# A one-core encoder kernel: the loads at the head of the RWKV-7 scan put in a hand-made order, and the last part of one gram step written earlier

## The chip, the cores and the metric

The kernel runs on one core of a Trainium2 chip. The metric is the device time of one execution in microseconds. Three runs of the kernel before took 2218.02, 2221.55 and 2223.59 us; the median is 2221.55 us. The profiled execution took 2221.22 us, and its program, from the first instruction to the last, spans 2219.4 us. All times of the trace are counted from the start of that span.

## What is computed

The reference is a two-layer encoder on 512 tokens of width 1024. Each layer is a half-step SwiGLU, a token mixer and another half-step SwiGLU, each followed by a layer norm. Layer 0 mixes by neighbourhood attention, layer 1 by a bidirectional RWKV-7 scan. The change lies in the mixer of layer 1:

```python
r = xr @ w_rkv[0]; k = xk @ w_rkv[1]; v = xv @ w_rkv[2]
g = jax.nn.sigmoid(xg @ g1) @ g2
...
def step(state, inp):
    r_t, w_t, k_t, v_t, a_t, b_t = inp
    sa = jnp.einsum('zbhij,zbhj->zbhi', state, a_t)
    state = state * w_t[..., None, :] + sa[..., None] * b_t[..., None, :] + v_t[..., None] * k_t[..., None, :]
    return state, jnp.einsum('zbhij,zbhj->zbhi', state, r_t)
_, ys = lax.scan(step, zeros, xs)      # one scan per direction z
...
return ((y + bonus) * g) @ w_out
```

`xr`, `xk`, `xv` and `xg` are token-shifted mixes of the input.

## The kernel before, in words

The work is fp32. The 16 heads of 64 channels are handled as 8 pairs (`hp`, 0 to 7), each 128 partitions wide. A scan over 512 tokens is cut into 8 chunks of 64 (`NC`), both directions `z` run side by side, and the recurrence inside a chunk is replaced by small matrices: products of keys and receptances ("grams"), the inverse of a triangular matrix per chunk, and then a chain over the 8 chunks that carries the state.

**Threads and slots.** `Scan.run` goes through slots `n` from -2 to 7. A slot holds threads, which are Python generators, and a string in the table `SEQ` says in which order their next parts are written out. For TensorE (PE), ScalarE (ACT) and VectorE (DVE) this written order is the order on the engine. The letters that matter here:

- `f0`, `f1`: `front`, the scaled receptances, keys and decays of pair n+3 in direction 0, or pair n+2 in direction 1. They write the tiles `ar0`/`ar1` (L1346, L1353) and `bk0`/`bk1` (L1360, L1363). One `ar` tile per direction exists, so the next pair's write to it has to wait until everything has read the old one.
- `g0`, `g1`: `grams`, six parts per pair and direction: for each half `q` of the chunks a PE part (L1385, masked out of PSUM by DVE at L1390), and then for each head `h` a part that copies pieces of the result to `qd` and `qc` on ACT (L1394, L1396) and issues two DMAs: L1397 moves a block of the unit `xs` to `az`, and L1398 puts a block of `ar` in its place in `xs`. The second one is what frees `ar`.
- `t0`, `t1`: `tails`, PE transposes of `bk` (L1408) that go to `tb` by ACT (L1409).
- `v`: `values`, `v = xv @ w_v` for one pair, one 128-row piece of the contraction per part (`a<-xv,wv` at L1063). `weigh` (L1431) loads the pair's weights `wv`.
- `r`: `receptances`, `r = xr @ w_r` for seven pairs, two pieces of the contraction per part (L1063, into the PSUM tiles `y` and `m` in turn), a copy by ACT (L1178) and a store to DRAM (L1179). Its inputs `xr` lie in `az2`, `xs8` and `xs9`, which nothing else uses yet; its weights lie in `xs4` to `xs7` and in two `vt` tiles. The first part of the thread (before slot -2) issues the loads of `xr` (L1148) and of the first weights.
- `q`: `gates`, four of the products with `g2`, each copied by ACT (L1441) into one of the tiles `yh`, `yt`, `gate`, `bon` and stored to DRAM by L1442.
- `b`: `bonus`; DVE L1448 reads the receptances and writes `kz`, PE makes a row sum of it, DVE L1453 reads that out of the PSUM tile `a` into `bon`. The tile `a` has two banks; `front` uses it too (L1327, and L270 to L272 for `a<-ah,a2u`).
- `i`, `k`, `j`: `invert` (one DVE transposition of `qd`, L1484, and then 62 POOL instructions, L1491 and L1493), `inverted` (DVE L1503 and L1512, which need POOL's result) and `merge` (PE L1524 and L1531). `c`, `d`: the chain over the chunks and its outputs.

**DMA order.** Every DMA here is issued by SP (SyncE). SP's order isn't written by hand: a scheduler puts the DMAs in line by its own estimate of when each is ready. `behind(x)` forces what stands inside to come after instruction `x` in that line. The eight loads of `xv` (256 KB each, L1161) are issued in the first `r` part of slot -2, after `wv` (L1431).

Of the kernel before, what the change touches and what calls it, by code (L numbers as in the profile page):

```python
# [18 lines left out]
P = 128  # L19
D = 1024  # L20
S = 512
FF = 2816
NF = FF // P
ND = D // P
# [34 lines left out]
}  # L59
SEQ = {  # L60
# [997 lines left out]
class Scan:  # L1058
# [76 lines left out]
    def receptances(self):  # L1135

        nc = self.nc
        one = lambda ap: ap.rearrange("p a b c d -> p (a b c d)")
        az = self.az[2].rearrange("p a b c -> p (a b c)")
        xr = [h[:, i * S : (i + 1) * S] for h, n in ((az, 4), (one(self.units[-2][0]), 2), (one(self.units[-1][0]), 2)) for i in range(n)]  # L1140
        w = {}

        def load(hp, ap):
            w[hp] = ap.rearrange("p (c f) -> p c f", c=ND)
            nc.sync.dma_start(w[hp], self.w_r[:, hp * P : (hp + 1) * P].rearrange("(c p) f -> p c f", p=P))

        def chunk(c):
            nc.sync.dma_start(xr[c], self.dram["xr"][:, c, :])  # L1148

        for n in ("mask", "onesb"):  # L1150
            nc.sync.dma_start(getattr(self, n), self.consts[n])
        chunk(0)
        for hp, i in zip(WR_FIRST, (4, 5, 6, 7)):
            load(hp, one(self.units[i][0]))
            if hp == WR_FIRST[0]:
                for c in range(1, ND):
                    chunk(c)
                self.weigh(0)
                yield
                for c in range(ND):  # L1160
                    nc.sync.dma_start(self.xv[:, c, :], self.dram["xv"][:, c, :])  # L1161
        for _ in range(2):
            self.unit()
        rest = [hp for hp in range(1, ND) if hp not in WR_FIRST]
        order = WR_FIRST + tuple(rest)
        while rest:
            pair, rest = rest[:2], rest[2:]
            vt = self.tile("vt", [P, NC, 2, 2, CH], 2)
            for i, hp in enumerate(pair):
                load(hp, one(vt)[:, i * D : (i + 1) * D])  # L1170
        for i, hp in enumerate(order):
            pr = self.k.bank("ym"[i % 2])
            for c in range(ND):
                self.wide(pr, w[hp][:, c, :], xr[c], c == 0, c == ND - 1)
                if c % 2 and c < ND - 1:
                    yield
            t = self.tile(("yh", "yt")[hp % 2], [P, S])
            nc.scalar.activation(t, pr, AF.Copy)  # L1178
            nc.sync.dma_start(self.dram["rkv"][0][:, hp, :], t)  # L1179
            if hp == order[-1]:  # L1180
                self.clear(2)
            yield
# [250 lines left out]
    def gates(self):  # L1433

        nc = self.nc
        for j, c in enumerate(range(ND - GATES, ND)):
            pg = self.k.bank("ym"[j % 2])
            for i, n in enumerate((P, 32)):
                nc.tensor.matmul(pg, self.g2[:n, i, j * P : (j + 1) * P], self.hidden[:n, i, :], start=i == 0, stop=i == 1)
            t = self.tile(("yh", "yt", "gate", "bon")[j], [P, S])  # L1440
            nc.scalar.activation(t, pg, AF.Copy)  # L1441
            nc.sync.dma_start(self.dram["g"][:, c, :], t)  # L1442
            yield

    def bonus(self, hp):
# [379 lines left out]
```

## Time and profile before

| | |
|---|---|
| three runs, us | 2218.02, 2221.55, 2223.59 (median 2221.55) |
| profiled execution, us | 2221.22 (span of the program 2219.4) |
| PE busy | 2180.0 us, 98% of the span |
| DVE, ACT, POOL busy | 1051.1, 957.7, 1413.1 us |
| mean granted TensorE clock | 0.994 |
| head of the scan | about 1414 to 1520 us (slots -2 and -1) |
| first slots with the chain over chunks | from about 1520 us |

The page's busy line says how long an engine had an instruction in work. The view of waits says, per waiting instruction line, what ended the wait, for how long in total, how often, and the longest one. A row of the timeline is: start, duration, engine, line, operation, output<-inputs by the program's tile names without their numbers, form, and how many equal instructions the row joins; in brackets how long the engine was idle before it and what released it. SPq rows are DMA issues by SP. An fp32 matmul instruction stands as two rows' worth of counts in the timeline (`x4` for two instructions). A row of the view by windows gives PE's busy time in that stretch, the count, the granted TensorE clock, the DMA engines' share and GB/s.

### The profile page before, as it was taken

The page shows a single profiled execution, that of the slowest core. Times are in us where ns is not written, and L with a number is a line of the kernel's source. Part 1 is how long each engine was busy: PE and PEld are TensorE (multiplying, and loading weights), DVE is VectorE, ACT ScalarE, POOL GpSimd, SP SyncE. Part 2 cuts the span into 40 slices and gives each one's busy share as a digit, 9 for nine tenths or more (in the row PEclk, how much of TensorE's full clock was granted, in tenths as well). Part 3 has the DMA queues.
Part 4 walks back from the last instruction along what each step waited for, and adds up shares of the span by engine and source line. Part 5 has one row for each costly group of instructions (what it writes and reads, how often), then busy time and mean ns, then how long its engine had stood idle before and what let it go on. Part 6 is the DMA issues. An engine that isn't in the chain of part 4 may idle for free. (4 is left out here: it accounts for less than half of the span.)

```text
span 2219.4 us, 35156 instructions
## 1 busy us (share of the span) xinstructions
PE 2180.0 (98%) x13834; PEld 1704.9 (77%) x13834; DVE 1051.1 (47%) x1526; ACT 957.7 (43%) x1678; POOL 1413.1 (64%) x1232
## 2 busy tenths in 40 slices
PE   9999999999999999999999999999999999999998
PEld 8888888887888888888888875445666657888886
DVE  3223355276433333633333588334788645333345
ACT  3333335377343333433333444336777533333333
POOL 5988855554487787488878542044777723887853
PEclk9999999999999999999999999999999999999999
DMA  7444463432344444454444645854444653444443
GB/s 206 147 155 144 142 223 100 136 89 91 103 138 143 150 147 150 150 181 146 143 138 142 209 130 181 277 142 129 128 129 120 194 162 102 151 142 142 138 171 123
DMA packets 350690, 329.15 MB, mean 148 GB/s; under 512 B 48491, under 2 KB 277483, under 8 KB 350525
## 3 DMA queue, kind: packets, MB, share of 16 engines
q1 hardware_dynamic: 350524, 326.91, 47.7%
q8 instruction: 109, 1.79, 0.3%
q14 instruction: 57, 0.46, 0.1%
HBM read 262.59 MB, written 47.74 MB: 140 GB/s over the span
## 5 line engine op out<-in xcount | busy, mean ns | idle before, releaser
L266 POOL TENSOR_TENSOR w<-raw,w 128x1024 fp32r<-128x1024 f32 (+1 forms) x202 | 499.7, 2475 | 255.4 <-ACT w L265 248.9
L270 PE MATMUL bank<-xT,w 128*128 128x512 f32 x1424 | 555.5, 390 | 0.0
L271 PE MATMUL bank<-xT,w 128*128 128x512 f32 x1424 | 554.2, 389 | 0.0
L272 PE MATMUL bank<-xT,w 128*128 128x512 f32 x1424 | 554.1, 389 | 0.0
L265 ACT ACTIVATE w<-raw 128x1024 fp32r<-128x1024 f32 (+1 forms) x206 | 217.3, 1057 | 318.0 <-PE bank L272 122.3
L477 DVE SCALAR_TENSOR_TENSOR ar<-bank,tmp 128x512 f32<-128x512 f32 x88 | 60.9, 692 | 563.9 <-PE bank L272 554.0
L272 PEld LDWEIGHTS bank<-xT,w 128*128 128x128 f32 x1424 | 267.3, 188 | 55.5
L270 PEld LDWEIGHTS bank<-xT,w 128*128 128x128 f32 x1424 | 267.4, 188 | 54.8
L271 PEld LDWEIGHTS bank<-xT,w 128*128 128x128 f32 x1424 | 267.4, 188 | 54.1
L871 PE MATMUL bank<-wx,an 128*128 128x512 f32 x792 | 187.3, 389 | 0.0
L1491 POOL TENSOR_TENSOR tm<-qs,zs 128x126 f32<-128x126 f32 (+22 forms) x248 | 105.5, 425 | 108.6 <-issue 48.3
L871 PEld LDWEIGHTS bank<-wx,an 128*128 128x128 f32 x792 | 148.7, 188 | 30.8
L871 PE MATMUL bank<-w,ring 128*128 128x512 f32 x720 | 168.8, 390 | 2.6 <-POOL w L266 2.6
L266 POOL TENSOR_TENSOR wx<-ra,wx 128x512 fp32r<-128x512 f32 x132 | 167.1, 1295 | 3.0 <-ACT wx L265 3.0
L266 DVE TENSOR_TENSOR ring<-ar,ring 128x1024 fp32r<-128x1024 f32 x44 | 121.3, 2757 | 90.2 <-ACT ring L265 90.1
L871 PEld LDWEIGHTS bank<-w,ring 128*128 128x128 f32 x720 | 134.9, 188 | 31.9 <-POOL w L266 3.6
L475 ACT ACTIVATE tmp<-bank 128x512 f32<-128x512 f32 x88 | 52.6, 598 | 231.5 <-PE bank L272 231.4
L1493 POOL TENSOR_TENSOR zs<-zs,tm 128x126 f32<-128x126 f32 (+22 forms) x248 | 113.9, 459 | 19.4
L265 ACT ACTIVATE wx<-ra 128x512 fp32r<-128x512 f32 x132 | 82.7, 633 | 79.0 <-PE bank L871 65.2
L266 POOL TENSOR_TENSOR w<-late,w 128x1024 fp32r<-128x1024 f32 x30 | 77.4, 2586 | 58.2 <-ACT w L265 58.2
L266 POOL TENSOR_TENSOR ring<-raw,ring 128x1024 fp32r<-128x1024 f32 x24 | 58.9, 2464 | 81.0 <-ACT ring L265 81.0
L270 PE MATMUL bank<-xT,ring 128*128 128x256 f32 (+1 forms) x304 | 87.3, 296 | 2.8 <-ACT xT L265 1.9
(315 smaller groups left out, 3714.3 us busy)
## 6 DMA issues: line engine op xcount, KB each, us to landing
raw<-in_ffn_w_in_dram SPq DMA_DIRECT2D x176, 512.0 KB, 3.9
ra<-in_ffn_w_out_dram SPq DMA_DIRECT2D x44, 1024.0 KB, 5.0
late<-d_late SPq DMA_DIRECT2D x34, 512.0 KB, 5.5
late<-in_ffn_w_out_dram SPq DMA_DIRECT2D x28, 512.0 KB, 4.4
raw<-in_w_qkv_dram SPq DMA_DIRECT2D x24, 512.0 KB, 3.9
d_late<-ts SPq DMA_DIRECT2D x44, 256.0 KB, 3.3
d_late<-ra SPq DMA_DIRECT2D x44, 256.0 KB, 2.0
xs<-ar SPq DMA_DIRECT2D x64, 128.0 KB, 2.4
```

Of the source, the lines that this page charges most:

```text
L265: self.hi = self.nc.scalar.activation(h, raw, AF.Copy).ins
L266: self.lo = (eng or self.nc.vector).tensor_tensor(l, raw, h.bitcast(F32), ALU.subtract).ins
L270: nc.tensor.matmul(out, wh, xh, start=start, stop=False)
L271: nc.tensor.matmul(out, wh, xl, start=False, stop=False)
L272: nc.tensor.matmul(out, wl, xh, start=False, stop=stop)
L475: nc.scalar.activation(s, pg, AF.Silu)
L477: nc.vector.scalar_tensor_tensor(raw[:, 3:7:3] if j else raw[:, 0:8:7], halves_of(pu), 0.5, halves_of(s), ALU.mult, ALU.mult)
L871: self.nc.tensor.matmul(acc, lhs, u[:, i], start=bool(first) and m == 0, stop=last and m == 2, skip_group_check=more)
L1491: nc.gpsimd.tensor_tensor(tv, qs[:, s, 0:s].rearrange("p (a o) -> p a o", o=1).broadcast_to([P, s, n]), zs[:, s : s + 1, c0:].broadcast_to ...
L1493: nc.gpsimd.tensor_tensor(zs[:, 0:s, c0:], zs[:, 0:s, c0:], tv, ALU.add)
```

## The change

Three edits. In `gates`, the four results go to the tiles `yt`, `gate`, `bon`, `yh` in this order (before: `yh`, `yt`, `gate`, `bon`), and the stores of the second to fourth are forced behind the last DMA remembered in `self.asked`. In `receptances`, the thread has one more stop: the load of `wv` and the eight loads of `xv` are issued in a part of their own, forced behind the first store of `gates`, and the last of the `xv` loads is what `gates` then stays behind. In `SEQ`, slot -2 calls that part between the first two `q`, takes all four parts of the first receptance product together before the second half of pair 0's grams, and slot -1 writes the last part of pair 1's `g0` right behind the part before it, where it stood much later, after the `g1` parts.

```diff
 SEQ = {
-    -2: "f1 q q f1 q f1 q g0 v f1 f1 f1 g0 l g0 r r g0 g0 v r g1 g1 g1 v r g1 v g1 g1 v t0 r g0 r r v f1 b r r t0 v r l v t1 "
+    -2: "f1 q r q f1 q f1 q g0 v f1 f1 f1 g0 l g0 r r r r g0 g0 v g1 g1 g1 v g1 v g1 g1 v t0 r g0 r r v f1 b r r t0 v r l v t1 "
        "i f0 r f0 r r v b f0 r r f0 r r t1 f0 r r f0",
-    -1: "f1 v g0 k f1 g0 g0 v r r f1 k r f1 f1 r j f1 g0 l l r g1 r n r g0 g1 f0 g1 j g1 f0 f1 r t0 g1 g1 n g0 v t0 v "
+    -1: "f1 v g0 k f1 g0 g0 v r r f1 k r f1 f1 r j f1 g0 l l r g1 r n r g0 g0 g1 f0 g1 j g1 f0 f1 r t0 g1 g1 n v t0 v "
        "f0 v v b f0 v t1 i f0 t1 f0 v n v r b",
...
             if hp == WR_FIRST[0]:
                 for c in range(1, ND):
                     chunk(c)
-                self.weigh(0)
                 yield
-                for c in range(ND):
-                    nc.sync.dma_start(self.xv[:, c, :], self.dram["xv"][:, c, :])
+                with self.k.behind(self.asked):
+                    self.weigh(0)
+                    for c in range(ND):
+                        self.asked = nc.sync.dma_start(self.xv[:, c, :], self.dram["xv"][:, c, :]).ins
+                yield
...
-            t = self.tile(("yh", "yt", "gate", "bon")[j], [P, S])
+            t = self.tile(("yt", "gate", "bon", "yh")[j], [P, S])
             nc.scalar.activation(t, pg, AF.Copy)
-            nc.sync.dma_start(self.dram["g"][:, c, :], t)
+            with self.k.behind(*[self.asked] if j else ()):
+                self.asked = nc.sync.dma_start(self.dram["g"][:, c, :], t).ins
             yield
```

What moves, engine by engine. POOL's and DVE's orders stay as they were. On SP at the head, before (tile numbers are kept here: `xs4_` to `xs9_` are units, `gh` holds k and iv of pair 1):

```order
L1148 DMA xs9_10657<-d_xr_71 128x512 x2
L1431 DMA wv_10693<-in_w_rkv_dram 128x8x128
L1442 DMA d_g_73<-yh_10650 128x512
L1442 DMA d_g_73<-yt_10649 128x512
L1442 DMA d_g_73<-gate_10652 128x512
L1290 DMA gh_10380<-d_k_69 128x512
L1292 DMA gh_10380<-d_iv_78 64x512
L1442 DMA d_g_73<-bon_10651 128x512
L1161 DMA xv_10639<-d_xv_72 128x512 x3
L1397 DMA az0_10668<-xs0_10655 64x4x64 x2
L1161 DMA xv_10639<-d_xv_72 128x512 x5
L1145 DMA xs5_10662<-in_w_rkv_dram 128x8x128
```

and with the change:

```order
L1148 DMA xs9_10657<-d_xr_71 128x512 x2
L1445 DMA d_g_73<-yt_10649 128x512
L1433 DMA wv_10703<-in_w_rkv_dram 128x8x128
L1162 DMA xv_10639<-d_xv_72 128x512 x8
L1445 DMA d_g_73<-gate_10652 128x512
L1445 DMA d_g_73<-bon_10651 128x512
L1445 DMA d_g_73<-yh_10650 128x512
L1399 DMA az0_10668<-xs0_10655 64x4x64
L1292 DMA gh_10380<-d_k_69 128x512
L1294 DMA gh_10380<-d_iv_78 64x512
L1399 DMA az0_10668<-xs0_10655 64x4x64
L1145 DMA xs5_10662<-in_w_rkv_dram 128x8x128
```

The loads of `xv` pass three of the gate stores, the loads into `gh` and the two moves to `az0`; the same DMAs as before stand ahead of `xs5`. On PE at the same place, before (`xs_10666` is `xs8`, `xs_10657` is `xs9`, `xs_10642` holds the first weights, `ar_10595` is direction 0 and `ar_10722` direction 1):

```order
L1063 MATMUL y<-az_10670,xs_10642 64x512 x8
L1385 MATMUL g<-ar_10595,bk_10596 128x128 x8
L1063 MATMUL a<-xv,wv 64x512 x2
L1063 MATMUL y<-xs_10666,xs_10642 64x512 x4
L1385 MATMUL g<-ar_10722,bk_10723 128x128 x8
L1063 MATMUL a<-xv,wv 64x512 x2
L1063 MATMUL y<-xs_10657,xs_10642 64x512 x4
L1385 MATMUL g<-ar_10722,bk_10723 128x128 x8
L1063 MATMUL a<-xv,wv 64x512 x4
L1408 MATMUL g<-ident,bk_10596 128x128 x4
```

and with the change:

```order
L1063 MATMUL y<-az_10670,xs_10642 64x512 x8
L1063 MATMUL y<-xs_10666,xs_10642 64x512 x4
L1063 MATMUL y<-xs_10657,xs_10642 64x512 x4
L1387 MATMUL g<-ar_10595,bk_10596 128x128 x8
L1063 MATMUL a<-xv,wv 64x512 x2
L1387 MATMUL g<-ar_10730,bk_10731 128x128 x8
L1063 MATMUL a<-xv,wv 64x512 x2
L1387 MATMUL g<-ar_10730,bk_10731 128x128 x8
L1063 MATMUL a<-xv,wv 64x512 x4
L1410 MATMUL g<-ident,bk_10596 128x128 x4
```

The two products that need neither `xv` nor `wv` now come ahead of the first one that does. On SP in slot -1, before (`ar0_11083` is pair 1's `ar0`):

```order
L1397 DMA az1_10669<-xs5_10662 64x4x64 x2
L1294 DMA a2r_11718<-in_a2_dram 128x2x128
L1179 DMA d_r_68<-yt_11283 128x512
L1398 DMA xs5_10662<-ar0_11083 64x512
L1397 DMA az1_10669<-xs6_10664 64x4x64 x2
L1398 DMA xs6_10664<-ar1_11197 64x512 x2
L1312 DMA lw_11820<-d_lw_77 128x4x128
L1397 DMA az1_10669<-xs7_10653 64x4x64 x2
L1398 DMA xs7_10653<-ar1_11197 64x512 x2
L1398 DMA xs5_10662<-ar0_11083 64x512
L1321 DMA g2_10381<-d_r_68 128x512
L1431 DMA wv_11578<-in_w_rkv_dram 128x8x128
```

and with the change:

```order
L1399 DMA az1_10669<-xs5_10662 64x4x64 x2
L1296 DMA a2r_11718<-in_a2_dram 128x2x128
L1181 DMA d_r_68<-yt_11283 128x512
L1400 DMA xs5_10662<-ar0_11083 64x512 x2
L1399 DMA az1_10669<-xs6_10664 64x4x64 x2
L1400 DMA xs6_10664<-ar1_11197 64x512 x2
L1314 DMA lw_11820<-d_lw_77 128x4x128
L1399 DMA az1_10669<-xs7_10653 64x4x64 x2
L1323 DMA g2_10381<-d_r_68 128x512
L1400 DMA xs7_10653<-ar1_11197 64x512 x2
L1433 DMA wv_11578<-in_w_rkv_dram 128x8x128
```

The last read of `ar0` moves from the end of this stretch to its first third, and the load `g2<-d_r` (receptances of a later pair) now stands ahead of the two copies into `xs7`. On ACT the three copies of that part (L1394 twice, L1396) move with it, from behind the copies of `xs7` to ahead of those of `xs6`; at the head the copy `yt<-y` (L1178) of the first receptance product comes ahead of the copies of `xs1`.

## The prediction

> **What bounds the kernel now.** I read the page's busy line first, then PE's waits in the stretch that the edits touch, then the timeline of each wait and the clock around it.
>
> ```profile
> PE 2180.0 (98%) x13834; PEld 1704.9 (77%) x13834; DVE 1051.1 (47%) x1526; ACT 957.7 (43%) x1678; POOL 1413.1 (64%) x1232
> ...
> PE a L1063 <- DMA xv<-d_xv: 5.0, 1, 5.0
> PE a L270 <- DVE bon L1453: 2.6, 1, 2.6
> PE p L1524 <- DVE qs L1512: 1.1, 1, 1.1
> ```
>
> PE is busy for 2180.0 of 2219.4 us and the edits take no instruction away, so they can only win PE's waits and what follows from them. Between 1400 and 1660 us PE has three waits of over 1 us, one each. Their sum, 8.7 us, is only part of their price, as the granted clock (fourth number) shows in the stretch of each wait and in the one behind it:
>
> ```profile
> 1429.45:1433.04 3.59, 0.00 (x0) 1.00 1.06 374
> 1433.04:1439.86 6.82, 5.38 (x14) 0.50 1.08 315
> 1521.78:1525.20 3.42, 0.83 (x17) 1.00 0.71 215
> 1525.20:1528.61 3.41, 3.41 (x23) 0.50 0.54 168
> 1552.50:1555.90 3.40, 2.21 (x96) 1.00 0.07 11
> 1555.90:1562.73 6.83, 6.83 (x54) 0.50 0.39 86
> ```
>
> Behind each wait PE runs at half clock for 3.4 or 6.8 us. A busy stretch at 0.50 loses about half its length: 5.38 x 0.5 = 2.7 us, 1.7 us and 3.4 us. So the three cost up to 5.0 + 2.7, 2.6 + 1.7 and 1.1 + 3.4 us. In the first pair of rows the DMA engines' share stands at 1.06 and 1.08: the head is bound by transfers, and what counts there is which transfer goes first.
>
> **The head (first two edits).** PE's rows from the wait on:
>
> ```profile
> 1434.48 1.97 PE L1063 MATMUL a<-xv,wv 128*64 128x512 f32 x4 [5.03 <-DMA xv<-d_xv]
> 1436.21 3.65 PE L1063 MATMUL y<-xs,xs 128*64 128x512 f32 x8
> 1439.79 1.18 PE L1385 MATMUL g<-ar,bk 64*128 64x128 f32 x16
> 1440.90 1.08 PE L1063 MATMUL a<-xv,wv 128*64 128x512 f32 x4
> 1441.81 1.89 PE L1063 MATMUL y<-xs,xs 128*64 128x512 f32 x8
> 1443.63 1.16 PE L1385 MATMUL g<-ar,bk 64*128 64x128 f32 x16
> 1444.72 1.94 PE L1063 MATMUL a<-xv,wv 128*64 128x512 f32 x8
> 1446.59 0.66 PE L1408 MATMUL g<-ident,bk 128*128 128x128 f32 x4
> 1447.17 3.65 PE L1063 MATMUL m<-az,xs 128*64 128x512 f32 x16
> ```
>
> PE was ready for the first `xv` piece at 1434.48 - 5.03 = 1429.45. From start to start at full clock, an `xv` part takes 0.91 us (1440.90 to 1441.81), a pair of receptance parts 1.82, a gram half 1.09, two `xv` parts 1.87, the transposes 0.58. With the change both receptance parts come first, so `xv` is wanted 2 x 1.82 later, at 1433.1. It also lands earlier. Ahead of the first `xv` load stood, after `xs9`, 512 KB of `wv`, four stores of 256 KB (three before, one just ahead), 256 KB into `gh` and 128 KB more; now one store and `wv`. That is 1152 KB less, 3.2 us at the 374 GB/s of the row above: 1434.5 - 3.2 = 1431.3. So it is there 1.8 us before it is wanted and the 5.0 us wait goes, with its half clock.
>
> What is late next? The weights `xs5`, used by `m<-az,xs`. The DMAs ahead of them are the same set as before, so I expect them to land when they did:
>
> ```profile
> L1145 SPq DMA_DIRECT2D xs<-in_w_rkv_dram x1: 383/383/383, 1436.7 to 1436.7; - x1
> ...
> DMA to landing us min/median/max: 5.8/5.8/5.8
> ...
> 1444.82 1.29 DVE L1390 TENSOR_TENSOR xs<-g,mask 128x512 f32<-128x512 f32 x2 [2.52 <-PE g L1385]
> ```
>
> Issue at 1436.7 plus 5.8 gives 1442.5. PE gets there at 1433.1 + 0.91 + 1.09 + 0.91 + 1.09 + 1.87 + 0.58 = 1439.55, and about 1.0 later because the gram halves now follow each other with a single `xv` part between them: the two banks come free 0.1 + 1.29 us after a half ends, the part covers 0.91 of it, so twice some 0.5 us remain. At 1440.55 PE waits 2.0 us for `xs5`. `m<-az,xs` starts at 1442.5 where it started at 1447.17: 4.65 us won. Does the new wait halve the clock? Bounds: nothing, or one stretch of 3.41 us, 1.7 us. The nearest row, the 2.6 us wait at 1525, paid that; 2.0 us is shorter, so I take 1.0. **The head wins 3.6 us** (1.0 if `xs5` lands 2 us late and the whole 1.7 is paid; 6.6 if it lands before 1440.55).
>
> The Trainium skill, "TensorE: Matmul & The Clock Gate", Part 1 (What's actually happening), says that the clock halves after at least one idle window of about 3.4 us, windows that run free of the program. The stretches of 3.41 and 6.82 us agree with such a window; the 2.6 us wait, shorter than it, halved the clock all the same. By the rule the new 2.0 us wait would cost no clock and the sum would be 1 us better; by the rows it costs part of a window.
>
> Of the other moves: three gate stores go out later, but their tiles are wanted only by later parts, and the store that goes first is that of `yt`, the tile that the first receptance product needs. The loads into `gh` (pair 1's k and iv) land some 6 us later (2.3 MB more ahead of them at 374 GB/s) and are first read by DVE at about 1470. These cost nothing as long as that slack holds.
>
> **Slot -1 (third edit).** The second wait is DVE's backlog. Columns as before; SPq rows are DMA issues.
>
> ```profile
> 1505.21 0.49 SPq L1398 DMA_DIRECT2D xs<-ar  x1
> 1513.89 1.76 SPq L1398 DMA_DIRECT2D xs<-ar  x3
> ...
> xs<-ar SPq DMA_DIRECT2D x40, 128.0 KB, 2.4
> ...
> 1505.35 0.60 ACT L1330 ACTIVATE e<-a 128x512 f32<-128x512 f32 x1
> ...
> 1517.63 0.74 DVE L1346 SCALAR_TENSOR_TENSOR ar<-k,cols,e 128x504 f32<-128x504 f32 x1 [10.88 <-ACT vt L1472]
> 1520.36 1.23 DVE L1484 STREAM_TRANSPOSE qs<-qd 128x1024 f32<-128x1024 f32 x1
> 1524.33 0.68 DVE L1453 TENSOR_TENSOR bon<-a,v 128x512 f32<-128x512 f32 x1
> ...
> 1525.07 0.70 PE L270 MATMUL a<-ah,a2u 128*128 128x512 f32 x1 [2.59 <-DVE bon L1453]
> ```
>
> DVE idles 10.88 us before it writes pair 2's `ar0`. The view names an ACT row, but the last of the three copies at 1513.89, issued at about 1515.1, is the last read of `ar0` and lands 2.4 us later, 1517.5. After that DVE works without a pause up to `bon`, for which PE waits. With the change that copy goes out right behind its twin of 1505.21, some 0.6 us later, and lands at about 1508.5; `e` is ready at 1505.95. So L1346 starts near 1509, 8.7 us earlier, and all that stands behind it on DVE moves up until it meets ACT's or PE's own times. Two parts follow:
>
> - `bon` is then bound by PE's own row sum, and L270's 2.59 us go, with the half-clock stretch of 1.7: **4.3 us** (2.6 if the clock drops there anyway).
> - L1484, which starts POOL's inversion, comes 8.7 us earlier too. This is the third wait:
>
> ```profile
> 1521.73 0.54 POOL L1491 TENSOR_TENSOR tm<-qs,zs 128x31 f32<-128x31 f32 x1 [19.61 <-issue]
> ...
> 1552.76 0.22 POOL L1493 TENSOR_TENSOR zs<-zs,tm 128x16 f32<-128x16 f32 x1
> ...
> 1553.02 1.04 DVE L1503 STREAM_TRANSPOSE qd<-zs 128x512 f32<-128x512 f32 x1 [2.46 <-POOL zs L1493]
> ...
> 1554.86 1.22 PE L1524 MATMUL p<-qs,qc 32*32 32x32 f32 x64 [1.12 <-DVE qs L1512]
> ```
>
> The inversion takes 31.3 us, and PE waits 1.12 us for its end. PE arrives 4.3 us earlier, POOL ends 8.7 us earlier: the 1.12 us wait had a lack of 1.1 and then has 8.7 - 4.3 - 1.1 = 3.3 us to spare. With its two half-clock windows it is worth **4.5 us** (1.1 if the clock drops there for another reason; the rows before it are small matmuls).
>
> The three ACT copies that move take 0.95 us, in an ACT that then idles 3 us for PE. `g2<-d_r` now stands ahead of the copies into `xs7` and must wait for DVE's L1448, the third row behind L1346: near 1510 that is no later than the copies went before.
>
> **The sum.** 3.6 + 4.3 + 4.5 = 12.4 us. The profiled execution took 2221.2 us, 0.3 below the median of the three runs, so I take it for typical: 2221.2 - 12.4 = 2208.8, rounded 2209 us.
>
> **Rivals.**
>
> - *The head only passes its wait on.* PE comes 7 us earlier to transfers that come no earlier; if `xs5` lands 2 us late and the clock drops for a window, the head wins 1.0: 1.0 + 4.3 + 4.5 = 9.8, 2211.4; with a second window 2213. For it: the DMA share of 1.08. Against: the same bytes stand ahead. Chance 0.15.
> - *`ar0` isn't what DVE waits for.* The row names ACT `vt`. Then the third edit does nothing: 2221.2 - 3.6 = 2217.6. Against: `vt` is no operand of L1346, and the copy's landing fits to 0.1 us. Chance 0.12.
> - *The clock doesn't notice the new wait* (the skill's rule): 2207.8. Of the three waits seen, all halved the clock. Chance 0.1.
> - *The third wait moves to pair 2.* POOL's next inversion can't start before the pair's last `qd` piece, so it gains less than PE does.
>
> ```profile
> 1556.06 0.60 POOL L1491 TENSOR_TENSOR tm<-qs,zs 128x31 f32<-128x31 f32 x1 [3.08 <-issue]
> ...
> 1588.84 0.69 POOL L1493 TENSOR_TENSOR zs<-zs,tm 128x16 f32<-128x16 f32 x1
> ...
> 1593.25 1.06 DVE L1503 STREAM_TRANSPOSE qd<-zs 128x512 f32<-128x512 f32 x1
> ```
>
>   It ends at 1589.5, 3.7 us before DVE wants it; of that PE's third gain takes up to 4.5, and an earlier POOL start gives at least 1 to 2 back. If the slack breaks, the 4.5 are lost: 2213.3. Chance 0.08.
> - *Slower.* At the head the copies that free `ar0` for pair 1 now stand behind `g2<-d_r` and, as before, behind six weight loads of 512 KB.
>
> ```profile
> 1458.29 2.53 SPq L1398 DMA_DIRECT2D xs<-ar  x4
> 1470.22 0.73 DVE L1346 SCALAR_TENSOR_TENSOR ar<-gh,cols,e 128x504 f32<-128x504 f32 x1
> ```
>
>   The second of the four landed near 1459 + 2.4 = 1461.4; one place later, 1462. DVE wants it at 1470.2 - 4.65 = 1465.6, so it decides only from there. Each microsecond beyond that holds DVE, and through `bk` PE. To eat 12.4 us it has to come after 1478, and at 1481 the time is 2224. Nothing in the profile holds SP that long. Chance 0.05.
>
> My forecast has 0.5. About 0.3% (6.7 us) is what a measurement of this kernel can tell from no change: faster means below 2214.9. The forecast, the first, third and fourth rival end below (0.83; I give 0.80, as the second windows of the clock fall by chance), the second within (same 0.14), slower 0.06. The range: the best head, 6.6 + 4.3 + 4.5 = 15.4, and a microsecond of scatter give 2204.5; the worst bounds together, 1.0 + 2.6 + 1.1 = 4.7, give 2216.5.
>
> **What would show it.** Right: no wait for `xv` in PE's waits; a wait of about 2 us for `xs<-in_w_rkv` in front of `m<-az,xs`, which starts near 1442.5; DVE's L1346 of pair 2 right after the copy lands, with some 2 us of idle before it where there were 10.9; no wait of L270 for `bon`, none of L1524 for `qs`; granted clock 1.00 from about 1446 to the end of slot 0. Wrong: a wait of over 4 us at `xs5`; L1346 still 10 us idle; a new wait for `qs` at pair 2.

## The result, and the profile after

| | median of runs | runs | profiled execution's span |
|---|---|---|---|
| before | 2222.78 us (2218.02 to 2224.51) | 8 | 2219.4 us |
| changed | 2212.14 us (2210.51 to 2217.03) | 8 | 2211.2 us |

The ratio is 0.9957, with a 95% interval of 0.9948 to 0.9966. The time lies inside the stated range (2204.5 to 2216.5 us): faster by 10.6 us between the medians, where 12.4 were forecast, and by 8.2 us between the two profiled executions. The profiled execution of the changed kernel took 2213.01 us as a whole, 0.9 above its median. The busy line of its page, and then PE's two longest waits in total between 1400 and 1660 us (us in total, times, longest):

```profile
PE 2177.1 (98%) x13834; PEld 1702.9 (77%) x13834; DVE 1058.3 (48%) x1526; ACT 957.5 (43%) x1678; POOL 1408.7 (64%) x1232
```

```profile
PE m L1063 <- DMA xs<-in_w_rkv_dram: 3.5, 1, 3.5
PE c L1555 <- DVE vt L1575: 0.8, 3, 0.3
```

The three waits of before, for `xv`, `bon` and `qs`, are gone. One new wait of 3.5 us stands in the head, for `xs5`, and no other is longer than 0.3 us. (Line numbers are 1 to 3 higher than before; from here on they are those of the kernel that is spoken of.)

The head in the timeline, with the load that it waits for (the DMA view: issue at 1437.8, 6.0 us from issue to landing), and the clock in PE's windows (us, PE busy, granted clock, DMA share, GB/s):

```profile
1439.78 0.66 PE L1410 MATMUL g<-ident,bk 128*128 128x128 f32 x4
1443.94 6.44 PE L1063 MATMUL m<-az,xs 128*64 128x512 f32 x16 [3.50 <-DMA xs<-in_w_rkv_dram]
```

```profile
L1145 SPq DMA_DIRECT2D xs<-in_w_rkv_dram x1: 389/389/389, 1437.8 to 1437.8; - x1
...
DMA to landing us min/median/max: 6.0/6.0/6.0
```

```profile
1442.77:1449.60 6.83, 5.66 (x14) 0.50 1.16 291
1449.60:1753.00 303.40, 298.23 (x4200) 1.00 0.52 136
```

PE got through its transposes at 1440.44, 0.1 before the forecast 1440.55. `xs5` landed at 1437.8 + 6.0 = 1443.8, 1.3 later than forecast, and the wait was 3.5 us instead of 2.0. The clock then halved for two windows, in which PE was busy for 5.66 us: some 2.8 us lost. That is why 16 matmuls `m<-az,xs` took 6.44 us here and 3.65 before. From 1449.6 on, the clock stands at 1.00 for 300 us: the halvings at 1525 and 1556 are gone.

Slot -1, in the timeline of DVE, POOL and PE:

```profile
1508.79 0.74 DVE L1348 SCALAR_TENSOR_TENSOR ar<-k,cols,e 128x504 f32<-128x504 f32 x1 [2.47 <-ACT qc L1398]
...
1511.51 1.24 DVE L1487 STREAM_TRANSPOSE qs<-qd 128x1024 f32<-128x1024 f32 x1
...
1512.88 0.24 POOL L1494 TENSOR_TENSOR tm<-qs,zs 128x31 f32<-128x31 f32 x1 [11.21 <-issue]
...
1519.84 0.69 DVE L1456 TENSOR_TENSOR bon<-a,v 128x512 f32<-128x512 f32 x1 [3.92 <-PE c L1555]
...
1521.73 0.50 PE L270 MATMUL a<-ah,a2u 128*128 128x512 f32 x1
...
1543.57 0.22 POOL L1496 TENSOR_TENSOR zs<-zs,tm 128x16 f32<-128x16 f32 x1
...
1546.30 1.06 DVE L1506 STREAM_TRANSPOSE qd<-zs 128x512 f32<-128x512 f32 x1
...
1549.38 1.20 PE L1527 MATMUL p<-qs,qc 32*32 32x32 f32 x64
```

DVE's idle time ahead of pair 2's `ar0` fell from 10.88 us to 2.47, and it starts at 1508.79 instead of 1517.63. The backlog behind it is gone: `bon` now follows 3.92 us of idle time and goes by PE's own rows, so L270 runs without a wait. POOL starts its inversion 8.85 us earlier (1512.88 for 1521.73) and ends it at 1543.79. DVE takes the result at 1546.30, so POOL has 2.5 us to spare, and L1527 waits for nothing.

What that left at the next pair, in the same view:

```profile
1582.95 0.22 POOL L1496 TENSOR_TENSOR zs<-zs,tm 128x16 f32<-128x16 f32 x1
...
1584.79 1.06 DVE L1506 STREAM_TRANSPOSE qd<-zs 128x512 f32<-128x512 f32 x1
```

POOL's slack of 3.7 us there shrank to 1584.79 - 1583.17 = 1.6 us and didn't break.

To set the runs side by side I cut each profile at four rows of PE: the first `y<-az,xs` of the head, the first `m<-az,xs`, and the first row sums `a<-kz,onesb` of three slots. "Head" is the stretch from the first to the first row sum, "slot" that from the second row sum to the third. All in us; the stretch between the first two row sums was 50.6 to 50.9 in all of them but the busy work (51.56) and `xs5` early (52.50).

| kernel | `y` to `m` | head | waits in the head | half clock in it | slot |
|---|---|---|---|---|---|
| before | 22.47 | 43.77 | `xv` 5.0 | 6.83 | 45.01 |
| changed | 18.99 | 43.09 | `xs5` 3.5 | 6.83 | 37.20 |
| changed, again | 19.25 | 42.99 | `xs5` 3.8 | 6.83 | 37.20 |
| head only | 18.81 | 41.58 | `xs5` 3.3 | 3.41 | 44.37 |
| slot only | 22.61 | 43.91 | `xv` 6.2 | 6.83 | 37.19 |
| `i` late | 18.95 | 40.25 | `xs5` 3.5 | none | 44.39 |
| loads only | 19.62 | 40.92 | `xv` 3.1 | 3.41 | 37.20 |
| PE order only | 19.73 | 41.03 | `xv` 3.3 | 3.41 | 37.19 |
| busy work | 19.25 | 40.55 | `xs5` 1.5 | none | 37.46 |
| `xs5` early | 15.42 | 36.72 | none | none | 37.19 |
| `xs5` early, tiles in turn | 15.43 | 36.73 | none | none | 37.19 |

Of the 8.2 us between the profiles of before and after, 7.8 lie in the slot and 0.7 in the head; the rest of the span gives 0.3 back.

### The profile page after: what moved, and what is told of

Read it like the earlier page. It is cut to its first block, busy times and chain, and to the rows that moved or that the text cites. A ratio compares the mean times of both kernels' runs of the same rounds, so it can differ in the third digit from the quotient of the medians.

```text
span 2211.2 us, 35159 instructions
## 1 busy us (share of the span) xinstructions
PE 2177.1 (98%) x13834; PEld 1702.9 (77%) x13834; DVE 1058.3 (48%) x1526; ACT 957.5 (43%) x1678; POOL 1408.7 (64%) x1232
## 4 chain that ended last, share of the span: by engine, by line
PE 86%; DVE 5%; DMA 4%; ACT 3%; issue 2%; POOL 1%; SPq 1%; DVEq 0%; ACTq 0%; POOLq 0%
PE bank L871 16%; PE bank L270 16%; PE bank L271 16%; PE bank L272 16%; PE bank L333 4%; PE a L1063 3%; PE g L1387 1%; PE m L1063 1%; DMA late<-in_ffn_w_out_dram 1%; PE y L1063 1%; PE bank L1253 1%; PE m L1573 1%; PE c L1555 1%; PE g L1063 1%; DVE ring L666 1%
## 5 line engine op out<-in xcount | busy, mean ns | idle before, releaser
L270 PE MATMUL bank<-xT,w 128*128 128x512 f32 x1424 | 555.5, 390 | 0.0
L270 PEld LDWEIGHTS bank<-xT,w 128*128 128x128 f32 x1424 | 267.3, 188 | 54.6
L483 DVE TENSOR_TENSOR ar<-ar 128x256 f32<-128x256 f32 x44 | 90.3, 2053 | 1.5
```

Of the source, the lines that this page charges most:

```text
L270: nc.tensor.matmul(out, wh, xh, start=start, stop=False)
L483: nc.vector.tensor_tensor(a(2), a(1), a(0), ALU.subtract)
```

## The experiments

The time before was measured anew beside each group: 2222.32 us (20 runs) for the first four, 2221.67 (14 runs) for those on the loads, on `i`, with the tiles in turn and for the changed kernel again, 2222.29 (9 runs) for PE's order alone.

**The head alone**: the changed kernel with slot -1 as before.

```diff
- ... r n r g0 g0 g1 f0 g1 j g1 f0 f1 r t0 g1 g1 n v t0 v
+ ... r n r g0 g1 f0 g1 j g1 f0 f1 r t0 g1 g1 n g0 v t0 v
```

> The head's edits alone, slot -1 as before. Theory (the three waits add up): the xv wait is gone and a wait of 2 to 3.5 us for xs5 stands in its place, the waits of L270 for bon (2.6 us) and of L1524 for qs (1.1 us) and their half-clock stretches are all still there; 1 to 4 us faster than before. Rival (the head's edits carry the whole gain): 8 us or more faster.

Measured: 2220.70 us (12 runs), ratio 0.9993 [0.9983, 1.0003]: 1.6 us, between 3.8 won and 0.7 lost. PE's waits of over 1 us, from 1400 to 1660:

```profile
PE m L1063 <- DMA xs<-in_w_rkv_dram: 3.3, 1, 3.3
PE p L1527 <- DVE qs L1515: 2.5, 1, 2.5
PE a L270 <- DVE bon L1456: 2.1, 1, 2.1
```

The new wait comes with the head's edits, and both later waits stay, of which the third has grown. One thing was not as expected: behind the wait for `bon` (2.1 us) the clock stayed at 1.00, and only behind the third wait did it halve, for two windows. The view by windows, from 1518.32 and from 1552.41:

```profile
1518.32:1521.73 3.41, 1.81 (x24) 1.00 0.84 255
1521.73:1525.15 3.42, 2.90 (x42) 1.00 0.51 161
...
1552.41:1555.83 3.42, 3.42 (x65) 0.50 0.33 52
```

The slot takes 44.37 us all the same, 0.6 less than before: what PE saves in clock at `bon` it waits longer for POOL.

**Slot -1 alone**: the kernel before with only the third edit (the diff above, reversed, on the kernel before).

> The edit of slot -1 alone, head as before. Theory: DVE writes pair 2's ar0 near 1509, as soon as the moved copy lands, the waits for bon and qs are gone, the 5 us wait for xv stays; 8 to 9 us faster than before. Rival (DVE waited for something else than ar0): no change, DVE's L1346 still near 1517.

Measured: 2214.42 us (8 runs), ratio 0.9964 [0.9952, 0.9976]: 7.9 us, where 8 to 9 were expected. Three quarters of the 10.6 come from this one part, moved. DVE's row for pair 2's `ar0`:

```profile
1509.57 0.74 DVE L1346 SCALAR_TENSOR_TENSOR ar<-k,cols,e 128x504 f32<-128x504 f32 x1 [1.98 <-DMA xs<-ar]
```

Here the releaser named is the copy `xs<-ar` itself. In the profile of before, the row named ACT `vt`, which L1346 doesn't read and which had ended at 1510.79, 6.8 us before L1346 started.

**`i` late**: the changed kernel, with pair 1's inversion started at the end of its slot, so that the gain of DVE's early `ar0` reaches everything but POOL.

```diff
-"f0 v v b f0 v t1 i f0 t1 f0 v n v r b"
+"f0 v v b f0 v t1 f0 t1 f0 v n v r b i"
```

> The changed kernel with the start of pair 1's inversion (the DVE transposition L1487 and POOL's 62 instructions) written as the last part of slot -1, behind bon; the same work. Theory (the third wait went because the inversion starts 8 us earlier): POOL starts near 1522 and ends near 1553, PE waits 4 to 6 us for qs at the first p<-qs,qc of the slot, with half clock behind it; 5 to 9 us slower than the changed kernel. Rival (the wait for qs was a follow-up of the wait for bon and needs no early inversion): the same time as the changed kernel within 2 us.

Measured: 2219.41 us (11 runs), ratio 0.9993 [0.9984, 1.0002], 7.3 us above the changed kernel in the same group (2212.09). POOL's first and last row of the inversion (timeline), PE's waits of over 1 us, and the clock at each wait (windows):

```profile
1517.54 0.24 POOL L1494 TENSOR_TENSOR tm<-qs,zs 128x31 f32<-128x31 f32 x1 [20.14 <-issue]
...
1547.36 0.22 POOL L1496 TENSOR_TENSOR zs<-zs,tm 128x16 f32<-128x16 f32 x1
```

```profile
PE p L1527 <- DVE qs L1515: 4.3, 1, 4.3
PE m L1063 <- DMA xs<-in_w_rkv_dram: 3.5, 1, 3.5
```

```profile
1438.98:1442.44 3.46, 0.00 (x1) 1.00 1.10 265
1442.44:1445.86 3.42, 3.42 (x16) 1.00 1.16 290
...
1549.70:1556.50 6.80, 6.80 (x103) 0.50 0.33 55
```

L270 doesn't wait, and yet almost nothing is won: PE now waits 4.3 us for POOL instead of 1.1, and loses 3.4 us of clock behind it as before. (POOL starts 3.1 us behind the second row sum here, where it started 2.4 behind it before, so 0.7 of the longer wait comes from the new place of `i`.) The slot takes 44.39 us against 45.01 before. From the second row sum to the first `p<-qs,qc` PE takes 35.5 us before, 35.0 with the head alone, where `bon` costs a wait but no clock, and 35.1 here, where it costs neither; in the changed kernel it takes 30.7. So as long as POOL ends late, POOL sets this stretch, whatever L270 costs. The second and third term of the sum were not two gains that stand side by side: the second is worth its 4.3 us only because the third edit also starts POOL earlier. The first two rows of the last fence hold something else: a wait of 3.46 us at `xs5`, as long as that of the changed kernel, with no halving of the clock behind it.

**The loads alone**: the changed kernel with PE's order in the head as before, SP's as changed.

```diff
-"f1 q r q f1 q f1 q g0 v f1 f1 f1 g0 l g0 r r r r g0 g0 v g1 g1 g1 v g1 v ...
+"f1 q r q f1 q f1 q g0 v f1 f1 f1 g0 l g0 r r g0 g0 v r g1 g1 g1 v r g1 v ...
```

> The changed kernel with PE's order in the head as before: the new order of loads and stores stays, the two receptance parts come between the xv parts again. Theory (what sets the end of the head is the landing of xs5, whichever work PE does first): PE waits 2 to 3 us for the first xv piece and 1 to 3 for xs5, m<-az starts within 0.7 us of where it starts in the changed kernel; the time is the changed kernel's within 2 us. Rival (PE's order carries the gain of the head): 3 us or more slower than the changed kernel.

**PE's order alone**: the kernel before with PE's new order in the head and the third edit, SP's load order in the head as before.

```diff
-"f1 q q f1 q f1 q g0 v f1 f1 f1 g0 l g0 r r g0 g0 v r g1 g1 g1 v r g1 v ...
+"f1 q q f1 q f1 q g0 v f1 f1 f1 g0 l g0 r r r r g0 g0 v g1 g1 g1 v g1 v ...
```

> The edit of slot -1 and PE's new order in the head, with the loads and stores of the head in the order of before. Theory (the landing of xs5 ends the head, whatever stands ahead of it): PE waits 1.5 to 2.5 us for the first xv piece and under 1 us for xs5, m<-az starts 18 to 19.5 us after y<-az,xs as in all the others but the kernel before; 8 to 11 us faster than before, within 2 us of the changed kernel. Rival (the new order of loads and stores is needed for the head's part): the time of the run with the edit of slot -1 alone, 7 to 8 us faster than before, with a wait of 5 us for xv.

Measured: 2212.65 us (5 runs), ratio 0.9957 [0.9944, 0.9970], for the loads; 2210.99 us (5 runs), ratio 0.9951 [0.9937, 0.9964], for PE's order. Their waits of over 1 us, the loads first:

```profile
PE a L1063 <- DMA xv<-d_xv: 3.1, 1, 3.1
```

```profile
PE a L1063 <- DMA xv<-d_xv: 3.3, 1, 3.3
```

Neither differs from the changed kernel (2212.09 and 2212.14) by more than 1.2 us. Either edit of the head cuts the wait for `xv` by about 2 us, and `m<-az,xs` then starts 19.6 or 19.7 us behind `y<-az,xs`; both together take that wait away, and `m<-az,xs` starts at 18.8 to 19.3. The two edits do not add up, since with both of them PE only meets the next load. The wait for `xs5` that was expected with the loads alone (1 to 3 us) did not come, and with PE's order alone the wait for `xv` was longer than expected (3.3 us, not 1.5 to 2.5) and `m<-az,xs` later (19.7, not 18 to 19.5): in both, `xs5` landed near 1443.9, 0.6 and 0.4 us before PE got there. So the landing of `xs5` leaves little to win in either. The medians lie 1.8 and 3.4 us below that of slot -1 alone, but the intervals of the ratios overlap.

**`xs5` early**: the changed kernel with the load of `xs5` between the fourth and the fifth `xv` load.

```diff
+if hp != WR_FIRST[1]:
     load(hp, one(self.units[i][0]))
...
+        if c == 3:
+            with self.k.behind(self.asked):
+                load(WR_FIRST[1], one(self.units[5][0]))
```

> The changed kernel with the load of xs5 moved up on SP to between the fourth and the fifth xv load, the gate stores behind the eight xv loads as they are. Theory (the head is bound by the order of transfers, and xs5 is the one that is late now): xs5 lands about 6 us earlier, near 1437, no wait of over 0.5 us is left in the head, m<-az starts near 1440.3, clock 1.00; 5 to 6.5 us faster than the changed kernel, 14 to 17 faster than before. Rival (the transfers as a whole are late, whichever goes first): the wait turns up at a later tile, xv or xs6, and the time is that of the changed kernel within 2 us.

Measured: 2211.76 us (5 runs), ratio 0.9954 [0.9939, 0.9970]. The head shrank from 43.0 us to 36.7, with no wait in it and no half clock. But the kernel's time is that of the changed kernel, within what these runs can tell: the 5 to 6.5 us that were expected did not come, and a new wait turned up further on, at a store and not at a load as the rival had it. PE, ACT and SP in the timeline:

```profile
1441.88 3.65 PE L1063 MATMUL m<-az,xs 128*64 128x512 f32 x16
...
1461.20 0.54 SPq L1185 DMA_DIRECT2D d_r<-yh  x1
...
1464.92 0.60 ACT L1184 ACTIVATE yh<-y 128x512 f32<-128x512 f32 x1 [6.60 <-DMA d_r<-yh]
1465.41 0.59 ACT L1430 ACTIVATE v<-a 128x512 f32<-128x512 f32 x1
...
1466.05 0.50 PE L270 MATMUL a<-ah,a2u 128*128 128x512 f32 x1 [1.84 <-ACT v L1430]
```

PE comes faster to a place where a store is still under way. ACT may write `yh` again only when the store `d_r<-yh`, issued at 1461.2, has landed; with that ACT's 6.6 us of idle time end, the copy of `v` queues behind it, and L270 waits 1.84 us for that. The stretch between the first two row sums took 52.50 us, 1.85 more than in the changed kernel. This explains 1.8 of the 6.3 us won in the head. Nor do the other 4.5 all show in the profile: its span, 2208.9 us, is 2.3 below that of the changed kernel's first profile and 0.8 below the second's. Against the first, the head begins 1.5 us later, and the stretch behind the slot is 0.7 longer; nothing here says whether that is more than scatter. The medians differ by some 0.4. The clock gives a hint: its mean was 0.999 in the profiled execution and 0.995 to 0.998 in the other four. Half-clock windows there would fit, but only the profiled execution has a trace, so this is not shown.

**`xs5` early, with the tiles in turn**: the same, and the copies of the receptances written to `yt` and `yh` alternately in the order in which they run (before, by their number `hp`, which runs 1, 4, 6, 7 there and put 4 and 6, one behind the other, into `yh`).

```diff
-t = self.tile(("yh", "yt")[hp % 2], [P, S])
+t = self.tile(("yt", "yh")[i % 2], [P, S])
```

> The early load of xs5 as in the run with xs5 moved up, and the receptance products go to the tiles yt and yh in strict turn, so that the third product's copy by ACT no longer waits for the store of the second. Theory (in that run the 6 us that the head won were partly given back, because ACT stood in this store's wait and so was late to empty the bank that L270 needs): no wait of L270 for ACT's v, from y<-az,xs to the first a<-kz,onesb some 36.7 us and from there to the second 50.7 us as in the changed kernel; 5 to 6.5 us faster than the changed kernel. Rival (the wait there comes from elsewhere): L270 still waits 1 to 2 us.

Measured: 2206.21 us (2204.63 to 2207.14, 5 runs), ratio 0.9928 [0.9914, 0.9942]. That is 15.5 us below the kernel before and 5.9 below the changed one in the same group: it beats both. ACT and PE in the timeline:

```profile
1440.98 3.65 PE L1063 MATMUL m<-az,xs 128*64 128x512 f32 x16
...
1459.97 0.60 ACT L1184 ACTIVATE yt<-y 128x512 f32<-128x512 f32 x1 [2.56 <-issue]
1462.49 0.60 ACT L1430 ACTIVATE v<-a 128x512 f32<-128x512 f32 x1 [1.93 <-PE a L1063]
```

ACT no longer waits for a store; `v` now waits for PE, and PE's longest wait from 1400 to 1660 is 0.4 us. The head keeps its 36.73, and the stretch behind it is back at 50.65. The mean clock is 0.998 or 0.999 in all five runs. The two kernels differ in this one line; between their medians lie 5.5 us, of which the profiles show 1.85 between the first two row sums.

**Busy work**: the changed kernel with ten products on the identity, whose results nobody reads, ahead of `m<-az,xs`, so that PE isn't idle while `xs5` is on its way.

```diff
 pr = self.k.bank("ym"[i % 2])
+if i == 1:
+    self.k.busy(pr, 10)
```

> The changed kernel with 10 more matmuls of the identity, which nothing reads, on PE just ahead of m<-az,xs5: some 2.4 us of work at full clock inside the wait for xs5. Theory (half of the price of the new wait is the clock behind it): the wait shrinks to about 1 us, m<-az starts when it did, and the granted clock stays at 1.00 behind it; 2 to 3 us faster than the changed kernel, 12 to 14 faster than before. Rival (the wait alone is the price): no faster than the changed kernel.

Measured: 2213.60 us (6 runs), ratio 0.9960 [0.9947, 0.9974]. PE in the timeline, and its two longest waits:

```profile
1439.78 2.40 PE L370 MATMUL m<-ident 128*128 128x128 f32 x20
...
1443.70 3.65 PE L1063 MATMUL m<-az,xs 128*64 128x512 f32 x16 [1.52 <-DMA xs<-in_w_rkv_dram]
```

```profile
PE m L1063 <- DMA xs<-in_w_rkv_dram: 1.5, 1, 1.5
PE a L270 <- ACT v L1428: 0.9, 1, 0.9
```

The work did what it should in the profile: `m<-az,xs` starts when it did, 19.25 us behind `y<-az,xs`, the clock stays at 1.00, and the head is 2.4 us shorter. 0.9 us go back at L270. In the median nothing is won where 2 to 3 us were expected, so as a way to a faster kernel this failed, and as a measure of the clock's price it stays inconclusive.

**The changed kernel again**, for the scatter of its profile.

> The changed kernel once more, to stand on the same chip beside the next three. Both theories: a wait of 2 to 3.5 us for xs5 and no other over 1 us; 9 to 11 us faster than before.

Measured: 2212.09 us (5 runs), ratio 0.9957 [0.9943, 0.9971], span 2209.7. The row that carries the head:

```profile
1443.25 6.09 PE L1063 MATMUL m<-az,xs 128*64 128x512 f32 x16 [3.75 <-DMA xs<-in_w_rkv_dram]
```

The wait of over 3 us and the two half-clock windows come again; the span differs by 1.5 us from the first profile.

## Why the prediction was right, and where a term was off

**The time and the sum.** 2209.0 forecast, 2212.1 measured. The mechanisms of all three terms were there. The slot's two terms were forecast at 8.8 us and came to 7.9 in the median of the kernel that has them alone, 7.8 in the profile. The head was forecast at 3.6 and came to 1.6 in the median of the kernel that has it alone (nothing isn't excluded) and 0.7 in the profile. The two medians give 9.5 of the 10.6; the missing 1.1 is within their intervals.

**The step that was mis-sized** is the head's "The DMAs ahead of them are the same set as before, so I expect them to land when they did", and the 1.0 us put down for the clock behind it. PE's arrival was right to 0.1 us, but `xs5` landed at 1443.8 and not at 1442.5. The forecast has `m<-az,xs` start 17.8 us behind `y<-az,xs`; in all five profiles with both of the head's edits and `xs5` in its old place it started 18.8 to 19.3 behind it, after a wait of 3.3 to 3.8 us, or 3.9 with the busy work counted in (2.40 + 1.52). The landing had been read off a single profile, in which `xs5` landed earlier against PE than in any later one that has the load in its old place and shows its landing (18.7 to 19.3 us behind `y<-az,xs`). It was issued 12.0 us behind `y<-az,xs` there and 13.0 in the kernel with slot -1 alone, whose head is the same. So "when they did" was off by 1.0 to 1.5 us for the typical case, and 2.0 us of wait was too little. The other part is the clock. The waits at `xs5` cost no window, one or two, and with them the head took 40.25, 41.58 and 43.0 to 43.1 us: 3.5, 2.2 and 0.7 us less than before. The 3.6 that were forecast is what the head wins when the clock doesn't notice; the changed kernel's two profiles show the dearest case. The bounds, 1.0 to 6.6, were meant for this and hold the median's 1.6; the profile's 0.7 falls just below.

**The rivals.** "The head only passes its wait on" (2211.4, or 2213 with a second window) is what the profile shows in the head: a wait of 3.5 us in place of one of 5.0, with two half-clock windows. It took the head from the forecast to its lower bound, and the measured time is nearer to this rival than to the forecast. The experiments show why: `xs5` lands 18.7 to 19.3 us behind `y<-az,xs`, whichever edit of the head is in, and `m<-az,xs` starts with it or at most 0.6 us later; moving that one load gives 6.3 us more. "`ar0` isn't what DVE waits for" has fallen: the third edit alone moved L1346 by 8 us, and there the profile names the copy; before and with the third edit alone, L1346 starts within 0.2 us of the landing of the last copy (issued at 1515.1 and 1507.1, 2.3 us to landing). "The third wait moves to pair 2" didn't happen; the slack fell from 3.7 us to 1.6, so the worry was sound and the price was not due. "Slower" has fallen with them. "The clock doesn't notice the new wait" did not come true here, where the wait cost two half-clock windows; with `i` late the same wait cost none.

**The slot, by its steps.** L1346 "near 1509": 1508.79. Some 2 us of idle ahead of it: 2.47. POOL's 3.3 us to spare: 2.5. What the prediction missed is that its second and third term hang together. With the inversion held back, `bon` no longer cost anything, and the third wait grew from 1.1 to 4.3 us with the same clock loss as before. The lower bounds that I gave them one by one (2.6 and 1.1) do not describe that case, in which the two together are worth 0.6 in the slot. Cut at the first `p<-qs,qc`, the 7.8 us are 4.85 ahead of it, where POOL's end sets the time, and 2.96 behind it, where the half clock had stood: the two waits and the clock at `bon`, priced at 2.6 + 1.1 + 1.7 = 5.4, and the clock of the third wait, priced at 3.4, both came out somewhat smaller.

**The clock.** The Trainium skill, "TensorE: Matmul & The Clock Gate", Part 1 (What's actually happening), says that the clock halves after at least one idle window of about 3.4 us, and that the windows run free of the program. The traces agree with the second half. The edges of the half-clock stretches lie on one grid: before the change it is 25 x 3.41 us from 1439.86 to 1525.20 and 8 x 3.41 from 1528.61 to 1555.90; with the head alone it is 31 x 3.41 from 1446.64 to 1552.41. And the grid stands differently against the program each time: in the two profiles of the changed kernel the clock halved 17.8 and 17.4 us behind `y<-az,xs`. The traces don't bear out the first half as a threshold: before the change, waits of 2.6 and 1.1 us, both shorter than a window, halved the clock, in windows in which PE was still busy for 0.83 and 2.21 us.

So what a wait costs in clock depends on how the edges split it. Here are windows of that grid that hold the wait for `xs5`: one of the changed kernel, one of the same kernel again, and the two of `i` late between which its wait of 3.46 us falls (the second number is PE's busy time):

```profile
1439.36:1442.77 3.41, 1.08 (x8) 1.00 1.09 224
...
1437.98:1441.39 3.41, 1.51 (x10) 1.00 0.94 232
...
1437.05:1440.46 3.41, 1.93 (x12) 1.00 0.99 210
1440.46:1443.87 3.41, 1.43 (x8) 1.00 1.16 292
```

The first two were followed by half clock, the last two were not; nor was the window of the head alone with 1.81 us of work, although PE waited 2.1 us for `bon` around its end. As 1.51 halved the clock and 1.43 did not, busy time alone isn't the whole rule. In the head, a second half-clock window came where the first still held over 1 us of the wait, and none where it held less. The same wait for `xs5` thus cost no half-clock window (3.46 us), one (3.31 us) or two (3.50 and 3.75 us), each of 3.41 us: that the changed kernel's two profiles paid the dearest price is chance, as far as these profiles tell.

## What to carry to other kernels

When a wait on a saturated queue is removed, ask which load ends the stretch, and move that one: here two edits each shortened the head by 2.7 to 2.9 us and did not add up, while moving the load `xs5` won 6 more. Before adding the prices of two waits in a row on one engine, check whether they end on different producers; here the early one was worth almost nothing without the late one, and both hung on one copy that stood too far back in SP's order. And ask what the faster stretch runs into: the 6 us won in the head showed in the time only when a tile that was still being stored had been taken out of the way.

## What was not expected of the hardware

- A wait's price in clock isn't a function of its length; it depends also on how the edges of windows of 3.41 us split the wait. Waits of 3.3 to 3.8 us at one place cost 0, 3.41 or 6.83 us at half clock in four profiles; waits of 3.1 and 3.3 us for `xv` cost 3.41, those of 5.0 and 6.2 cost 6.83. A single profile can thus be off by up to 2.8 us on the clock alone, a third of the 8.2 us between the two profiles.
- The heads of the changed kernel and of the one with `xs5` early differ by 6.3 us in the profiles (43.0 and 36.7), the spans by 0.8 or 2.3, and the medians by some 0.4. The profile of one execution and the median of several answer different questions, and in such a case the median decides.
- The releaser that a row names can be wrong where a DMA is the cause: at 10.88 us of idle time the trace named ACT `vt`, which had ended 6.8 us earlier, and only in the kernel with the third edit alone did it name the copy.
